# Down products with partial sums kept in PSUM, low parts of four passes on VectorE, and token block sums ordered a pair ahead

## The chip, the cores and the metric

The kernel runs on one core of a Trainium2 chip. The metric is the device time of one execution in microseconds (us). Five engines work side by side, each through its own queue in order: TensorE (PE in the rows; PEld is its weight load), VectorE (DVE), ScalarE (ACT), GpSimd (POOL) and SyncE (SP), which here issues the DMAs.

## The reference

A hybrid encoder layer is run on two request groups of 1024 tokens with the same weights. What matters here is its feed-forward end, per group:

```python
xn = rms_norm(h, norm_ffn_g[l])
g, u = jnp.split(xn @ w_gate_up[l], 2, axis=-1)      # 1024 x 1024 @ 1024 x 5632
h = h + (jax.nn.silu(g) * u) @ w_down[l]             # 1024 x 2816 @ 2816 x 1024
h = rms_norm(h, final_norm_g)
```

All is float32.

## The kernel before

**Products.** A float32 operand is split into a high part, rounded to the matmul's 32-bit format (`fp32r`), and a low part, the rest. `mm3` (line 430) makes one product of 128x128 by 128x512 out of three matmuls: high by high, high by low, low by high. ScalarE makes the high part (a CAST), VectorE or GpSimd the low part (a subtraction), both into one operand tile `wop`.

**Seven products for eight.** The gate and up products and the down products are cut into 2 x 2 blocks, and the four block results come from seven block products by Winograd's scheme. Its price is sums: of token blocks (`t23`, in `x_side`), of weight blocks, of hidden activation blocks `A[i, j, c]` (i the token half, j even or odd hidden tile), and of results.

**The down products.** `DN` lists the seven passes. A pass is 11 units (`c` from 0 to 10), one for each pair of hidden tiles of 128; a unit is four token quarters `q` by three matmuls, into the four PSUM banks of the pass, so 132 matmuls a pass. The banks of even and of odd passes alternate. When a pass is through, `C[p]` says into which blocks of `h` (token half, column half) its banks are added; `dn_unit` spreads these additions (`add`, VectorE, one 128x512 each, PSUM and SBUF in, SBUF out) over the units of the next pass, behind the quarters 1 and 3; in P3 at most two a unit. When none is left in P3, `T.d_free` is set, and the PSUM banks go to what follows: the transposes of the next group's tokens (`nx_trans`) in the first group, the final norms of the odd row tiles in the second.

**Operands of a unit.** `prep_dn` takes the sums of activation and weight blocks (VectorE; two of them by turns on VectorE and GpSimd, `turn`) and lets ScalarE make the two high parts, of the activation operand `sop` and the weight operand `top`. `prep_dn_lo` makes the low part of `top` on VectorE and that of `sop` on GpSimd. `prep(n)` is called ahead of unit n: it prepares further units as long as the operand tiles suffice (a ring of 7, 6 of them in use, 2 a unit, so up to unit n + 2), and then `lows(n + 2)` makes the low parts up to unit n + 1. That is the order in every engine's queue: sums and high parts of unit n + 2, low parts of unit n + 1, additions beside unit n. `trun` holds one block of `w_down` that is changed in place from pass to pass; `raws` holds the other blocks, loaded by SP into four buffers, each one when the load four before it is freed.

**Token block sums.** `x_side` is a generator that TensorE's program steps between groups of three matmuls of the first gate and up products. Of each of four token quarters it transposes blocks by TensorE (`x_trans`: four 128x128 transposes into one PSUM bank, then ScalarE's high part and VectorE's low part). B22 comes first; then, quarter by quarter, the sums `t23` (two VectorE operations, the second on the first), two GpSimd operations on `b21` and `b12`, and the transposes of T2, T3 and T4, T4 being the block that GpSimd wrote.

All instructions carry the line of the helper that emits them (line 120), so rows are told apart by tiles: `aA` to `aV` hold activation blocks, `wraw` a block of weights, `t` is `t23`, `x2n` the normed tokens.

Of the kernel before, what the change touches and what calls it, by code (L numbers as in the profile page):

```python
# [37 lines left out]
DN = ("P1", "P2", "P4", "P5", "P7", "P6", "P3")  # L38
# [208 lines left out]
def hymba_kernel(ctx, tc, ins, outs, dbg=None):  # L247
# [891 lines left out]
    def attention(T, b):  # L1139
# [341 lines left out]
        def x_side():  # L1481
# [37 lines left out]
            for q in range(4):  # L1519
                x_trans("B22", q, blocks(q)[3])  # L1520
                yield True
            for q in range(4):
                b11, b21, b12, b22 = blocks(q)
                t23 = slot(("s6", "s2")[q % 2], [P, 2, 512], name="t23")
                dve.tensor_tensor(t23[:, 1], b22, b12, ALU.subtract)
                dve.tensor_tensor(t23[:, 0], t23[:, 1], b11, ALU.add)
                yield True
                pool.tensor_tensor(b21, t23[:, 0], b21, ALU.subtract)
                pool.tensor_tensor(b12, b12, b11, ALU.subtract)
                x_trans("T2", q, t23[:, 0])  # L1530
                yield True
                x_trans("T3", q, t23[:, 1])
                yield True
                x_trans("T4", q, b21)
                yield True
# [76 lines left out]
    def ffn_stream(T, b):  # L1612
# [33 lines left out]
        two("P2", 1, L0)  # L1646
        for c in range(NC):
            items.append((("P4", c), [P, 2, 512], [(lambda r, i=i: r[:, i], rows(2 * c + i, L1)) for i in range(2)]))
        for c in range(NC):
            items.append((("P5", c), [P, 2, 512], [(lambda r: r.rearrange("p a b -> p (a b)"), rows(2 * c, slice(0, D)))]))  # L1650
        two("P6", 0, L0)
# [54 lines left out]
        def trun_tile(c):  # L1706
            if c % 2 == 0:
                trun[c // 2] = slot(trun_tags[c // 2], [P, 2, 512], name="trun")
                for i in range(min(2, NC - c)):
                    sync.dma_start(out=trun[c // 2][:, i], in_=rows(2 * (c + i), L0))  # L1710
# [6 lines left out]
        def prep_dn(p, c):  # L1717
            tr = trun[c // 2][:, c % 2]
            turn = (dve, pool)[c % 2]
            if p == "P1":  # L1720
                src, s = tr, A[1, 1, c]
            elif p == "P2":
                src, s = raws[(p, c - c % 2)][:, c % 2], A[1, 2, c]
                dve.tensor_tensor(tr, tr, src, ALU.subtract)
            elif p == "P4":
                r = raws[(p, c)]
                b12, b22 = r[:, 0], r[:, 1]
                dve.tensor_tensor(b22, b22, b12, ALU.subtract)
                turn.tensor_tensor(b12, b22, tr, ALU.add)
                src, s = b12, A[2, 2, c]  # L1730
            elif p == "P5":
                r = raws[(p, c)]
                dve.tensor_tensor(A[2, 2, c], A[2, 1, c], A[2, 2, c], ALU.add)
                dve.tensor_tensor(r[:, 0], r[:, 1], r[:, 0], ALU.subtract)
                src, s = r[:, 0], A[2, 2, c]
            elif p == "P7":
                dve.tensor_tensor(A[2, 1, c], A[1, 1, c], A[2, 1, c], ALU.subtract)
                src, s = tr, A[2, 1, c]
                dve.tensor_tensor(A[1, 1, c], A[2, 2, c], A[1, 1, c], ALU.subtract)
            elif p == "P6":  # L1740
                r = raws[(p, c - c % 2)]
                dve.tensor_tensor(tr, tr, r[:, c % 2], ALU.add)
                src, s = tr, A[1, 1, c]
            else:
                src, s = raws[(p, c - c % 2)][:, c % 2], A[1, 2, c]
# [5 lines left out]
            if p == "P6":  # L1751
                turn.tensor_tensor(A[1, 2, c], A[1, 2, c], A[1, 1, c], ALU.subtract)
            half[p, c] = src, s, sop, top

        def prep_dn_lo(p, c):
            src, s, sop, top = half.pop((p, c))
            dve.tensor_tensor(top[:, 1], src, fv(top[:, 0]), ALU.subtract)
            pool.tensor_tensor(sop[:, 1], s, fv(sop[:, 0]), ALU.subtract)
            ops["dn", p, c] = (q4((sop[:, 0], sop[:, 1])), (top[:, 0], top[:, 1]))
            if p in ("P2", "P6", "P3"):  # L1760
                if c % 2 or c == NC - 1:
                    freed.add((p, c - c % 2))
            elif p in ("P4", "P5"):
                freed.add((p, c))

# [34 lines left out]
    def ffn(T, b, nxt):  # L1800
# [112 lines left out]
        def gu_hook(p, t):  # L1913
# [5 lines left out]
            if p == "P1":  # L1919
                a_load(1, 1, 0, slot(xb[0], [P, 8, 512], name="aA"), 0, 8)  # L1920
# [272 lines left out]
```

## Time and profile before

| | us |
|---|---|
| median of 3 runs (lowest to highest) | 2489.55 (2488.89 to 2494.42) |
| the profiled execution | 2492.62 |
| its span, first to last instruction | 2490.8 |
| TensorE busy in it | 2356.5 |
| down products, first group | 1012.7 to 1252.0 |
| down products, second group | 2244.2 to 2476.5 |

Times in rows count from the start of the span. A matmul's listed duration overlaps the next one's, so the pace is read from starts: a unit of 12 matmuls takes about 2.8 us. The mean granted clock of TensorE is 0.983 of full speed.

### The profile page before, as it was taken

Reading aid. Unit: us, or ns where it says so; the run is one execution under the profiler, and the core shown is the slowest. Engines: PE = TensorE matmul, PEld = TensorE weight load, DVE = VectorE, ACT = ScalarE, POOL = GpSimd, SP = SyncE. Lnnn points to the kernel's source line nnn. Section 1 sums busy time; section 2 is a strip of 40 time slices with the busy share of each in tenths; the row PEclk is TensorE's granted clock in tenths of the full one; section 3 lists DMA queues with packets and bytes.
Section 4 is the critical chain, followed back from the end, with each engine's and each line's share of the span. In section 5 each row is a group of like instructions: output and inputs, shape, how many; then the busy total and the mean of one; then the engine's idle time right before and its main releaser. Section 6 shows DMA issues by size and latency. Waiting matters only on the chain. (4 is left out here: it accounts for less than half of the span.)

```text
span 2490.8 us, 34160 instructions
## 1 busy us (share of the span) xinstructions
PE 2356.5 (95%) x12458; PEld 1992.5 (80%) x12458; DVE 1775.0 (71%) x2472; ACT 1187.2 (48%) x2131; POOL 1256.0 (50%) x1156
## 2 busy tenths in 40 slices
PE   7998999998999999999989889999899999999997
PEld 7887899877888888777777789988778888887765
DVE  6686888876555555599966778888755555557996
ACT  4476667664232222343545766666532232223434
POOL 5323666544444444466663156665444444444665
PEclk9999999999999999999999999999999999999999
DMA  5113000111222222842430130001212223247513
GB/s 140 39 37 103 18 18 18 43 68 43 85 85 85 76 77 93 337 151 70 144 130 21 37 108 22 10 18 43 85 51 77 85 77 93 77 140 283 169 47 114
DMA packets 189704, 212.78 MB, mean 85 GB/s; under 512 B 24272, under 2 KB 141008, under 8 KB 188512
## 3 DMA queue, kind: packets, MB, share of 16 engines
q1 hardware_dynamic: 189536, 210.60, 26.1%
q8 instruction: 98, 1.61, 0.3%
q14 instruction: 70, 0.57, 0.1%
HBM read 168.45 MB, written 39.85 MB: 84 GB/s over the span
## 5 line engine op out<-in xcount | busy, mean ns | idle before, releaser
L120 PE MATMUL dn<-wop 128*128 128x512 f32 x1848 | 449.4, 401 | 17.7 <-DVE wop L120 14.5
L120 PEld LDWEIGHTS dn<-wop 128*128 128x128 f32 x1848 | 343.2, 189 | 117.0 <-DVE wop L120 36.4
L120 POOL TENSOR_TENSOR pexp<-pexp,rsum 128x1024 f32<-128x1024 f32 x128 | 242.9, 1898 | 230.6 <-DVE rsum L120 158.4
L120 PE MATMUL gu<-xT,wop 128*128 128x512 f32 x1344 | 352.1, 394 | 0.0
L120 POOL TENSOR_TENSOR wop<-wraw,wop 128x512 fp32r<-128x512 f32 x176 | 228.9, 1302 | 214.1 <-ACT wop L120 214.1
L120 PEld LDWEIGHTS gu<-xT,wop 128*128 128x128 f32 x1344 | 252.7, 188 | 57.9
L120 POOL TENSOR_TENSOR wop<-wsum,wop 128x512 fp32r<-128x512 f32 x126 | 163.1, 1294 | 256.1 <-ACT wop L120 256.1
L120 PE MATMUL gu<-xB,wop 128*128 128x512 f32 x1136 | 287.8, 396 | 0.7 <-DVE xB L120 0.6
L120 ACT CAST wop<-wraw 128x512 fp32r<-128x512 f32 x264 | 162.2, 617 | 208.7 <-DVE wraw L120 127.2
L120 PE MATMUL gu<-xH,wop 128*128 128x512 f32 x1056 | 254.8, 396 | 0.0
L120 PEld LDWEIGHTS gu<-xB,wop 128*128 128x128 f32 x1136 | 212.1, 188 | 47.9 <-ACT xB L120 1.1
L120 PEld LDWEIGHTS gu<-xH,wop 128*128 128x128 f32 x1056 | 198.1, 188 | 46.0
L120 ACT CAST pt<-ptp 128x512 fp32r<-128x512 f32 x256 | 148.9, 586 | 121.2 <-PE ptp L120 119.9
L120 DVE TENSOR_REDUCE m<-S 128x1 f32<-128x1041 f32 x128 | 158.1, 1235 | 56.2 <-PE S L120 55.4
L120 ACT ACTIVATE pexp<-S,m 128x1041 f32<-128x1041 f32 x128 | 145.0, 1133 | 67.4 <-DVE m L120 59.8
L120 DVE TENSOR_TENSOR pt<-ptp,pt 128x512 fp32r<-128x512 f32 x256 | 168.2, 681 | 5.3 <-ACT pt L120 4.3
L120 PE MATMUL ptp<-idf,pexp 128*128 128x128 f32 x1024 | 156.4, 277 | 10.2 <-DVE pt L120 6.6
L120 PE MATMUL pvo<-pt,vst 128*128 128x256 f32 x1024 | 155.3, 295 | 3.5 <-DVE attnT L120 3.5
L120 PE MATMUL S<-kh,qs 128*128 128x348 f32 (+1 forms) x384 | 137.5, 360 | 21.9 <-ACT pexp L120 15.6
L120 PEld LDWEIGHTS ptp<-idf,pexp 128*128 128x128 f32 x1024 | 126.0, 143 | 21.5 <-issue 7.9
L120 ACT CAST wop<-wsum 128x512 fp32r<-128x512 f32 x126 | 78.0, 619 | 135.2 <-DVE wsum L120 135.2
L120 DVE SCALAR_TENSOR_TENSOR act<-th,act 128x512 f32<-128x512 f32 x84 | 139.0, 1654 | 2.9
(292 smaller groups left out, 5186.0 us busy)
## 6 DMA issues: line engine op xcount, KB each, us to landing
wraw<-in_w_gate_up SPq DMA_DIRECT2D x176, 256.0 KB, 3.8
wraw<-in_w_down SPq DMA_DIRECT2D x110, 256.0 KB, 3.0
ad<-act SPq DMA_DIRECT2D x44, 512.0 KB, 3.5
wraw<-in_w_down SPq DMA_DIRECT2D x22, 512.0 KB, 3.3
wraw<-in_w_in SPq DMA_DIRECT2D x32, 256.0 KB, 3.6
hd<-h SPq DMA_DIRECT2D x16, 512.0 KB, 5.0
h<-hd SPq DMA_DIRECT2D x16, 512.0 KB, 10.2
out<-h SPq DMA_DIRECT2D x15, 512.0 KB, 2.8
```

What stands on the lines that cost most here:

```text
L120: return fn(*args, **kw)
```

## The change

The down products run in another order, P2, P1, P4, P6, P5, P7, P3, and three of them (P6, P7, P3: `onto`) start on the banks of the pass two before them and add to what stands there: P6 onto P1, P7 onto P1 + P6, P3 onto P5. `C` has fewer entries for that. The sums of activations and weights are arranged anew, all on VectorE; in P4, P5, P6 and P7 the low part of `sop` is VectorE's too, elsewhere GpSimd's. P2 now takes its weights from `trun`, which is loaded with the odd rows; P1 and P7 load the even ones. The first activations loaded are those of odd hidden tiles. In `x_side` the sums of quarter q + 1 are issued ahead of the transposes of quarter q. The diff; the loads of activations, which change places in it as their passes do, are left out:

```diff
--- before.py
+++ after.py
@@ -35,7 +35,7 @@
 GU = (("P1", "B11"), ("P6", "T2"), ("P2", "B21"), ("P7", "T3"), ("P5", "T1"), ("P4", "T4"), ("P3", "B22"))
 
 FIRST = {"A11": ("B11", "B12"), "A21": ("B11", "B12"), "A12": ("B21", "B22"), "A22": ("B21", "B22")}
-DN = ("P1", "P2", "P4", "P5", "P7", "P6", "P3")
+DN = ("P2", "P1", "P4", "P6", "P5", "P7", "P3")
 NC = NHT // 2
 
 GELU_A = 0.044715
@@ -1519,19 +1519,26 @@
             for q in range(4):
                 x_trans("B22", q, blocks(q)[3])
                 yield True
+            t23 = {}
+
+            def sums(q):
+                b11, b21, b12, b22 = blocks(q)
+                t = t23[q] = slot(("s6", "s2")[q % 2], [P, 2, 512], name="t23")
+                dve.tensor_tensor(t[:, 1], b22, b12, ALU.subtract)
+                dve.tensor_tensor(t[:, 0], t[:, 1], b11, ALU.add)
+                pool.tensor_tensor(b21, t[:, 0], b21, ALU.subtract)
+                pool.tensor_tensor(b12, b12, b11, ALU.subtract)
+
+            sums(0)
+            yield True
             for q in range(4):
-                b11, b21, b12, b22 = blocks(q)
-                t23 = slot(("s6", "s2")[q % 2], [P, 2, 512], name="t23")
-                dve.tensor_tensor(t23[:, 1], b22, b12, ALU.subtract)
-                dve.tensor_tensor(t23[:, 0], t23[:, 1], b11, ALU.add)
-                yield True
-                pool.tensor_tensor(b21, t23[:, 0], b21, ALU.subtract)
-                pool.tensor_tensor(b12, b12, b11, ALU.subtract)
-                x_trans("T2", q, t23[:, 0])
-                yield True
-                x_trans("T3", q, t23[:, 1])
-                yield True
-                x_trans("T4", q, b21)
+                if q < 3:
+                    sums(q + 1)
+                    yield True
+                for i, n in enumerate(("T2", "T3")):
+                    x_trans(n, q, t23[q][:, i])
+                    yield True
+                x_trans("T4", q, blocks(q)[1])
                 yield True
             while not T.b12_free:
                 yield False
@@ -1643,12 +1650,13 @@
                 items.append(((p, c), [P, 2, 512], [
                     (lambda r, i=i: r[:, i], rows(2 * (c + i) + j, cs)) for i in range(min(2, NC - c))]))
 
-        two("P2", 1, L0)
+        two("P1", 0, L0)
         for c in range(NC):
             items.append((("P4", c), [P, 2, 512], [(lambda r, i=i: r[:, i], rows(2 * c + i, L1)) for i in range(2)]))
+        two("P6", 0, L0)
         for c in range(NC):
             items.append((("P5", c), [P, 2, 512], [(lambda r: r.rearrange("p a b -> p (a b)"), rows(2 * c, slice(0, D)))]))
-        two("P6", 0, L0)
+        two("P7", 0, L0)
         two("P3", 1, L1)
         freed = set()
 
@@ -1707,7 +1715,7 @@
             if c % 2 == 0:
                 trun[c // 2] = slot(trun_tags[c // 2], [P, 2, 512], name="trun")
                 for i in range(min(2, NC - c)):
-                    sync.dma_start(out=trun[c // 2][:, i], in_=rows(2 * (c + i), L0))
+                    sync.dma_start(out=trun[c // 2][:, i], in_=rows(2 * (c + i) + 1, L0))
 
         T.trun_tile = trun_tile
 
@@ -1716,52 +1724,54 @@
 
         def prep_dn(p, c):
             tr = trun[c // 2][:, c % 2]
-            turn = (dve, pool)[c % 2]
-            if p == "P1":
-                src, s = tr, A[1, 1, c]
-            elif p == "P2":
-                src, s = raws[(p, c - c % 2)][:, c % 2], A[1, 2, c]
-                dve.tensor_tensor(tr, tr, src, ALU.subtract)
+            r = None if p == "P2" else raws[(p, c if p in ("P4", "P5") else c - c % 2)]
+            rc = None if p == "P2" else r[:, c % 2]
+            if p == "P2":
+                src, s = tr, A[1, 2, c]
+            elif p == "P1":
+                src, s = rc, A[1, 1, c]
             elif p == "P4":
-                r = raws[(p, c)]
                 b12, b22 = r[:, 0], r[:, 1]
                 dve.tensor_tensor(b22, b22, b12, ALU.subtract)
-                turn.tensor_tensor(b12, b22, tr, ALU.add)
+                dve.tensor_tensor(b12, b22, tr, ALU.add)
                 src, s = b12, A[2, 2, c]
+                if c >= NC // 2:
+                    dve.tensor_tensor(A[2, 1, c], A[2, 1, c], A[2, 2, c], ALU.add)
+            elif p == "P6":
+                if c < NC // 2:
+                    dve.tensor_tensor(A[2, 1, c], A[2, 1, c], A[2, 2, c], ALU.add)
+                dve.tensor_tensor(A[1, 1, c], A[2, 1, c], A[1, 1, c], ALU.subtract)
+                dve.tensor_tensor(tr, tr, rc, ALU.add)
+                src, s = tr, A[1, 1, c]
             elif p == "P5":
-                r = raws[(p, c)]
-                dve.tensor_tensor(A[2, 2, c], A[2, 1, c], A[2, 2, c], ALU.add)
                 dve.tensor_tensor(r[:, 0], r[:, 1], r[:, 0], ALU.subtract)
-                src, s = r[:, 0], A[2, 2, c]
+                dve.tensor_tensor(A[2, 2, c], A[2, 2, c], A[1, 1, c], ALU.subtract)
+                src, s = r[:, 0], A[2, 1, c]
             elif p == "P7":
-                dve.tensor_tensor(A[2, 1, c], A[1, 1, c], A[2, 1, c], ALU.subtract)
-                src, s = tr, A[2, 1, c]
-                dve.tensor_tensor(A[1, 1, c], A[2, 2, c], A[1, 1, c], ALU.subtract)
-            elif p == "P6":
-                r = raws[(p, c - c % 2)]
-                dve.tensor_tensor(tr, tr, r[:, c % 2], ALU.add)
-                src, s = tr, A[1, 1, c]
+                dve.tensor_tensor(rc, tr, rc, ALU.subtract)
+                dve.tensor_tensor(A[1, 1, c], A[1, 2, c], A[1, 1, c], ALU.subtract)
+                src, s = rc, A[2, 2, c]
             else:
-                src, s = raws[(p, c - c % 2)][:, c % 2], A[1, 2, c]
+                src, s = rc, A[1, 1, c]
             sop, top = op_tile(), op_tile()
             act.copy(sop[:, 0], s)
             act.copy(top[:, 0], src)
             if p == "P4":
                 act.copy(tr, r[:, 1])
-            if p == "P6":
-                turn.tensor_tensor(A[1, 2, c], A[1, 2, c], A[1, 1, c], ALU.subtract)
             half[p, c] = src, s, sop, top
 
         def prep_dn_lo(p, c):
             src, s, sop, top = half.pop((p, c))
             dve.tensor_tensor(top[:, 1], src, fv(top[:, 0]), ALU.subtract)
-            pool.tensor_tensor(sop[:, 1], s, fv(sop[:, 0]), ALU.subtract)
+            (dve if p in ("P4", "P5", "P6", "P7") else pool).tensor_tensor(sop[:, 1], s, fv(sop[:, 0]), ALU.subtract)
             ops["dn", p, c] = (q4((sop[:, 0], sop[:, 1])), (top[:, 0], top[:, 1]))
-            if p in ("P2", "P6", "P3"):
-                if c % 2 or c == NC - 1:
-                    freed.add((p, c - c % 2))
-            elif p in ("P4", "P5"):
+            if p == "P1":
+                tr = trun[c // 2][:, c % 2]
+                dve.tensor_tensor(tr, src, tr, ALU.subtract)
+            if p in ("P4", "P5"):
                 freed.add((p, c))
+            elif p != "P2" and (c % 2 or c == NC - 1):
+                freed.add((p, c - c % 2))
 
         n_lo = [0]
 
...
-        C = {"P1": ((1, 1, 1), (1, 2, 1), (2, 1, 1), (2, 2, 1)), "P2": ((1, 1, 1),), "P3": ((1, 2, 1),),
-             "P4": ((2, 1, -1),), "P5": ((1, 2, 1), (2, 2, 1)), "P6": ((1, 2, 1), (2, 1, 1), (2, 2, 1)),
-             "P7": ((2, 1, 1), (2, 2, 1))}
+
+        C = {"P2": ((1, 1, 1),), "P1": ((1, 1, 1),), "P4": ((2, 1, -1),), "P6": ((1, 2, 1),), "P5": ((2, 2, 1),),
+             "P7": ((2, 1, 1), (2, 2, 1)), "P3": ((1, 2, 1),)}
+        onto = ("P6", "P7", "P3")
         adds = []
         banks = {}
 
@@ -1963,11 +1974,11 @@
         def dn_unit(p, c):
             n = DN.index(p)
             if c == 0:
-                banks[n] = [bank(n % 2, q, "dn") for q in range(4)]
+                banks[n] = banks[n - 2] if p in onto else [bank(n % 2, q, "dn") for q in range(4)]
             (sh, sl), (th, tl) = ops.pop(("dn", p, c))
             due = -(-len(adds) // (NC - c)) if p != "P3" else min(2, len(adds))
             for q in range(4):
-                mm3(banks[n][q], sh[:, q], sl[:, q], th, tl, c == 0, c == NC - 1)
+                mm3(banks[n][q], sh[:, q], sl[:, q], th, tl, c == 0 and p not in onto, c == NC - 1, p in onto)
                 if q % 2 and due:
                     due -= 1
                     adds.pop(0)()
@@ -2059,10 +2070,10 @@
                     need(*guards[u])
                 elif T.x_in[guards[u][0]] < guards[u][1]:
                     return False
-            if u[0] == "dn" and u[1] == "P1":
-                return (1, 1, u[2]) in A
+            if u[0] == "dn" and u[1] == "P2":
+                return (1, 2, u[2]) in A
             if nxt is not None and u[0] == "dn":
-                if u[1:] == ("P6", NC - 3):
+                if u[1:] == ("P7", NC - 3):
                     T.no_rope = True
                 if u[1:] == ("P3", 1):
                     nxt_begin()
```

## Rows read from the trace of the kernel before

**Rows 1.** The page: busy us, share of the span and instructions of each engine.
```profile
PE 2356.5 (95%) x12458; PEld 1992.5 (80%) x12458; DVE 1775.0 (71%) x2472; ACT 1187.2 (48%) x2131; POOL 1256.0 (50%) x1156
```

**Rows 2.** Windows by pass: stretch, its us, busy us (instructions) by engine, clock, DMA share, GB/s.
```profile
core 0: us, PE busy (x) PEld busy (x) DVE busy (x) ACT busy (x) POOL busy (x), PEclk, DMA share, GB/s
...
1076.61:1109.58 32.97, 31.36 (x134) 24.60 (x132) 32.83 (x33) 16.70 (x30) 23.74 (x15) 1.00 0.49 161
1109.58:1141.54 31.96, 31.96 (x134) 23.97 (x132) 31.89 (x38) 13.48 (x23) 16.67 (x12) 1.00 0.55 179
1141.54:1178.41 36.87, 34.80 (x133) 25.10 (x132) 36.56 (x42) 13.30 (x24) 24.17 (x15) 0.95 0.05 16
1178.41:1211.74 33.33, 31.83 (x134) 24.27 (x132) 31.25 (x35) 12.13 (x21) 19.13 (x14) 1.00 0.34 111
...
2279.03:2309.60 30.57, 30.57 (x134) 24.81 (x132) 27.32 (x39) 13.61 (x24) 15.08 (x11) 1.00 0.50 188
2309.60:2342.49 32.89, 31.38 (x133) 24.58 (x132) 32.75 (x33) 16.71 (x30) 23.71 (x15) 1.00 0.50 160
2342.49:2374.45 31.96, 31.96 (x133) 24.01 (x132) 31.89 (x38) 13.47 (x23) 16.67 (x12) 1.00 0.55 180
2374.45:2409.80 35.35, 33.30 (x134) 23.96 (x132) 35.04 (x41) 13.08 (x24) 22.82 (x14) 1.00 0.01 2
2409.80:2445.80 36.00, 32.45 (x133) 24.13 (x132) 34.66 (x37) 12.78 (x23) 22.35 (x16) 1.00 0.24 81
```

**Rows 3.** Timeline of VectorE in P4, second group: start, us, operation, [idle before].
```profile
2317.12 0.67 DVE L120 TENSOR_TENSOR h<-h,dn 128x512 f32<-128x512 f32 x1
2317.72 0.68 DVE L120 TENSOR_TENSOR wraw<-wraw 128x512 f32<-128x512 f32 x1
2318.32 0.68 DVE L120 TENSOR_TENSOR wop<-wraw,wop 128x512 fp32r<-128x512 f32 x1
2318.92 0.68 DVE L120 TENSOR_TENSOR h<-h,dn 128x512 f32<-128x512 f32 x1
2319.52 1.18 DVE L120 TENSOR_TENSOR wraw<-wraw 128x512 f32<-128x512 f32 x1
2320.74 1.66 DVE L120 TENSOR_TENSOR wraw<-wraw,trun 128x512 f32<-128x512 f32 x1
```

**Rows 4.** Timeline of GpSimd in the same stretch.
```profile
2318.53 1.62 POOL L120 TENSOR_TENSOR wraw<-wraw,trun 128x512 f32<-128x512 f32 x1 [1.88 <-DVE wraw L120]
2320.11 1.73 POOL L120 TENSOR_TENSOR wop<-aC,wop 128x512 fp32r<-128x512 f32 x1
```

**Rows 5.** Timeline of VectorE and of ScalarE in P2, second group.
```profile
2293.82 0.69 DVE L120 TENSOR_TENSOR wop<-wraw,wop 128x512 fp32r<-128x512 f32 x1 [0.39 <-ACT wop L120]
...
2293.17 0.62 ACT L120 CAST wop<-wraw 128x512 fp32r<-128x512 f32 x1 [1.65 <-PE dn L120]
```

**Rows 6.** Timeline of TensorE at the start of the second group's down products.
```profile
2244.15 3.21 PE L120 MATMUL dn<-wop 128*128 128x512 f32 x13
2249.86 3.35 PE L120 MATMUL dn<-wop 128*128 128x512 f32 x7 [2.51 <-DVE wop L120]
```

**Rows 7.** Timeline of TensorE, VectorE, GpSimd at the token block sums.
```profile
574.71 0.63 PE L120 MATMUL tp<-idf,t 128*128 128x128 f32 x4 [1.42 <-DVE t L120]
...
591.86 0.63 PE L120 MATMUL tp<-idf,t 128*128 128x128 f32 x4 [1.41 <-DVE t L120]
...
1823.82 0.63 PE L120 MATMUL tp<-idf,t 128*128 128x128 f32 x4 [1.41 <-DVE t L120]
...
573.88 0.69 DVE L120 TENSOR_TENSOR t<-t,x2n 128x512 f32<-128x512 f32 x1
...
574.71 1.28 POOL L120 TENSOR_TENSOR x2n<-t,x2n 128x512 f32<-128x512 f32 x1 [4.28 <-DVE t L120]
```

**Rows 8.** Timeline of TensorE around the end of the first group's P3.
```profile
1228.74 0.60 PE L120 MATMUL tp<-idf,xn 128*128 128x128 f32 x4
...
1255.37 0.47 PE L120 MATMUL pin<-xsXH,whi 128*128 128x512 f32 x1 [3.42 <-DVE h L120]
```

**Rows 9.** Timeline of VectorE behind the last matmul.
```profile
2479.13 2.47 DVE L120 SCALAR_TENSOR_TENSOR h<-h,rs,gfin 128x1024 f32<-128x1024 f32 x2
2482.32 1.28 DVE L120 SCALAR_TENSOR_TENSOR h<-h,rs,gfin 128x1024 f32<-128x1024 f32 x1 [0.72 <-POOL rs L120]
```

More of the change, by code (lines that the diff above doesn't have):

```diff
@@ L1919, in gu_hook @@
             if p == "P1":
-                a_load(1, 1, 0, slot(xb[0], [P, 8, 512], name="aA"), 0, 8)
+                a_load(1, 2, 0, slot(xb[0], [P, 8, 512], name="aA"), 0, 8)
                 T.trun_tile(2)
@@ L1923, in gu_hook @@
                 hold["B"] = slot(xb[1], [P, 8, 512], name="aB")
-                a_load(1, 1, 8, hold["B"], 0, 2)
+                a_load(1, 2, 8, hold["B"], 0, 2)
             elif p == "P2":
@@ L1933, in gu_hook @@
                 hold["V"] = v4
-                a_load(1, 2, 0, w, 0, 2)
-                a_load(1, 2, 2, s7, 0, 2)
+                a_load(1, 1, 0, w, 0, 2)
+                a_load(1, 1, 2, s7, 0, 2)
             elif p == "P3":
@@ L1938, in gu_hook @@
                     T.trun_tile(c)
-                a_load(1, 1, 10, hold["B"], 2, 1)
+                a_load(1, 2, 10, hold["B"], 2, 1)
                 k4, s5 = (slot(x, [P, 2, 512], name="aS") for x in (S_K, "s5"))
-                a_load(1, 2, 4, k4, 0, 2)
-                a_load(1, 2, 6, s5, 0, 1)
-                a_load(1, 2, 7, hold["V"], 0, 4)
+                a_load(1, 1, 4, k4, 0, 2)
+                a_load(1, 1, 6, s5, 0, 1)
+                a_load(1, 1, 7, hold["V"], 0, 4)
                 h = T.h = slot("H", [P, TT, D], name="h")
```

## The prediction

> **What bounds the kernel now.** I read the page first: TensorE is busy for 95% of the span, VectorE for 71% [rows 1]. So a gain can come only from the places where TensorE waits, or runs slower than its clean pace. The change touches two stages, the down products (seven passes of 11 units, 132 matmuls a pass) and the token block sums in front of the gate and up products, so I cut these stages out: a table of windows by pass for the first, the timeline for the second.
>
> The passes [rows 2]. P2 of the second group runs without a wait: 30.57 us, 2.78 a unit. I take that as the clean pass (the same pass of the first group took 30.49); four of them are 122.2. The passes P4, P5, P7, P6 take 32.97 + 31.96 + 36.87 + 33.33 = 135.1 us in the first group and 32.89 + 31.96 + 35.35 + 36.00 = 136.2 in the second: 12.9 and 14.0 too much. In each of the eight, VectorE is busy nearly as long as the pass (31.89 of 31.96 in P5), while TensorE has idle time: VectorE is the bound there.
>
> But is it by its own work? Its timeline says no [rows 3]. While GpSimd stands still, one VectorE operation of 128x512 starts every 0.60 us (2317.12, 2317.72, 2318.32, 2318.92), though each is listed with 0.67 to 0.68. At 2318.53 GpSimd starts [rows 4]; the VectorE operation at 2319.52, with both inputs in SBUF, now takes 1.18 instead of 0.68: the GpSimd one ends at 2318.53 + 1.62 = 2320.15, and VectorE's 0.55 later, as if it had waited for that end. The next one, beside the GpSimd operation of 2320.11, takes 1.66. The two engines take turns. In P5 of the second group 38 operations fill 31.89 us, 0.84 each; without turns they would be 38 x 0.60 = 23. An addition that reads PSUM (`h<-h,dn`) isn't lengthened.
>
> **The change part by part.** *Fewer additions.* With the sums kept in PSUM, the list of additions to `h` shrinks from 14 block products x 4 = 56 to 8 x 4 = 32 a group. At 0.60 that is 14 us of VectorE a group, no time of TensorE by itself.
>
> *Low parts on VectorE.* In P4, P6, P5, P7 GpSimd loses all it did there: 44 low parts and 10 sums a group. VectorE gets them. Its operations in these four passes, by the new `prep_dn`: P4 22 sums, 6 of A, 22 low parts; P6 5 + 22 and 22; P5 and P7 22 and 22 each; 16 additions to `h`. That is 203 operations a group. At 0.60 they are 122 us, against 122.2 of the clean matmuls: by the whole, a draw. So order decides. An operation that reads what the one before it wrote starts 0.04 after the listed end (2319.52 + 1.18, then 2320.74 [rows 3]): 0.72 for the first of such a pair.
>
> By the order written, a step holds the sums of two units on, the low parts of the next, and one addition in the first four steps. In P4: 0.72 + 0.60 + 1.20 + 0.60 = 3.12 for three steps, 3.72 for the fourth (the A sum starts at c = 5), then 3.12, where the last two hold P6's sums: 34.9 us against 30.6, so 4.3 short. In P6: 0.72 + 1.20 + 1.20 + 0.60 = 3.72 for three steps, 3.00 for one, then 2.40: short by 3 x 0.94 + 0.22 = 3.0, then faster than TensorE by 0.38 a step. In P5 and P7: 3.00 for four steps (0.9 short in all), then 2.40.
>
> What covers this is VectorE's lead. In P2's pass it works as far ahead as the ring of operand tiles lets it: ScalarE's copy at 2293.17 had waited for TensorE, and the low part behind it starts at 2293.82 after 0.39 of idle time [rows 5]. By the units of 2.78 from 2279.03, the fifth unit had then just ended; the ring gives its tile to the unit three on, the eighth, which starts at 2298.5. So a low part is ready 4.0 us early. P4 uses that up and lacks 0.3 to 0.6; P6 pays its 3.0 in full; P5 and P7 live on the regained lead. Loss: 3.6 us a group, so 125.8 for the four. Bounds: nothing (122.2), and 8 if there is no lead at all. Gain: 135.1 - 125.8 = 9.3 and 136.2 - 125.8 = 10.4, together **19.7**, bounds 11 and 27.
>
> *The moved waits.* P6, P7 and P3 start onto banks that VectorE has to have read; those additions lie in the first four units of the pass between, seven units earlier: nothing. If VectorE were seven units late, that would be priced above already. P7 loads B11 a second time, 11 blocks of 256 KB a group on SP's queue; in the pass P7 of before the DMA engines are busy for 0.01 of the time [rows 2], and each load waits for a raw buffer four loads back, so nothing. The stop of 2.51 us in the second unit of the whole stage [rows 6] is VectorE's and GpSimd's turns at the end of the gate products; P2 as first pass has the same operations as P1 had, and I leave it at zero, between -2 and +2.
>
> *Token block sums.* Before, each of the four sums of a group is issued right ahead of the transposes that need it: TensorE stands for 1.42 us until the second of the two dependent VectorE operations is done [rows 7]; four times in each group, the first and the last shown. After, a sum is issued three or four transposes ahead. Only the first has no lead, but one step of three matmuls (3 x 2.78 / 12 = 0.7) more in front of it: about 0.7 of its 1.42 stays. Gain 4 x 1.42 - 0.7 = 5.0 a group, **10.0**; bounds 6 and 11.4. What could be late next is the third transpose of each four, which reads a GpSimd result: it ended 574.71 + 1.28 - 574.57 = 1.4 after its sum, with VectorE taking turns perhaps 2.0 (1.73 there [rows 4], against 1.28 here), and the third transposes come three steps, 2.1, and two transposes after that: still in time.
>
> *The two ends.* With 8 instead of 12 additions at two a unit the banks for what follows come free after four units of P3 and not after six, 5.6 us earlier. In the first group the transposes of the next group's tokens start at 1228.74 and the next products wait 3.42 us for the last additions [rows 8]; VectorE would then reach those additions sooner. I take **2.5**, between 0 and 5: it can't be more than the wait and the small stops around it. In the second group the odd rows are finished earlier, and the row of two operations at 2479.13 [rows 9] holds one fewer: **0.9**, between 0 and 1.5.
>
> The sum: 19.7 + 10.0 + 2.5 + 0.9 = **33.1 us**. The profiled execution took 2492.62, so 2459.5; it is 3.1 above the median of the runs, from which it would be 2456.5. I take **2458**.
>
> A rule against this: the Trainium skill, "VectorE: DVE Perf Modes", section "The DRAIN you can't avoid", says that the next operation starts only when the pipe of the one before is empty (a section beside it lets some start earlier). By it an operation would cost its whole listed time, and the trace doesn't agree: 0.68 listed, 0.60 from start to start. It is the first rival.
>
> **The rivals.**
> - *VectorE at its listed time.* 203 operations at 0.68 are 138.0 a group; less the 4.0 of lead, 134.0 against 135.1 and 136.2. The passes give 3 us, the rest stands: 2492 - 17 = about 2475. For it: the listed durations, and that many of the new operations have another order than the ones read. Against it: every undisturbed row.
> - *Slower: a chain of waits.* VectorE has to wait for ScalarE's copy between sums and low parts. If it does so with its lead gone, every operation costs 0.72 or more, as the dependent pair does, and there is no lead: 2 x 146.2 against 271.3 is 21 more, less 13.4 from the other parts: 8 slower, **2498**. It decides from 0.70 us an operation on. For it: P4 and P6 run without lead for ten steps. Against it: between a unit's sums and its low parts stand the low parts of another, 1.2 us or more, and ScalarE's two copies are 1.05.
> - *The sums bring nothing,* since the third transpose then waits for GpSimd, whose operations take turns with the sum ahead: 10 less, 2468. Against it: the 2.0 against over 2.1 above; it is close, so the chance isn't small.
> - *No loss in the passes and all ends at their best:* 2445 to 2448.
> - *The change doesn't do what it says* (low parts still on GpSimd) is excluded by the code for P4 to P7; P2, P1 and P3 keep theirs.
>
> **How the numbers follow.** The forecast 0.66; the sums bring nothing 0.12; the best case 0.08; listed time 0.07; the chain of waits 0.07. The range takes the first three and part of the fourth: 2445 to 2477. A change under 0.2% (5 us) is about what a measurement of this kernel can't tell from none. Slower: the chain and a little for what I don't see, 0.08. Same: 0.04, the upper end of listed time. Faster: 0.88.
>
> **What would show it.** After: the passes P4, P6, P5, P7 at about 31, 33.5, 30.6, 30.6 with GpSimd idle in them; VectorE starts 0.60 apart; TensorE's stops, if any, in the first units of P6 and waiting for VectorE; no 1.42 before the transposes but a 0.7 in front of the first; transposes in P3 from its fifth unit on. Wrong if P5 and P7 take over 31.5 (VectorE is slower than 0.60), or if transposes wait for GpSimd.

## The result and the profile after

| | before | changed |
|---|---|---|
| median of 4 runs, us | 2489.22 (2488.33 to 2494.42) | 2458.85 (2456.95 to 2461.70) |
| ratio to before | 1 | 0.9877, 95% interval 0.9864 to 0.9889 |
| span of the profiled execution, us | 2490.8 | 2458.2 |

The kernel is 30.4 us faster; 2458 was forecast. First the windows by pass of the changed kernel, as in [rows 2]: P4, P6 of the first group (P5 and P7 took 30.52 and 30.55), then P4, P6, P5, P7 of the second.

```profile
core 0: us, PE busy (x) PEld busy (x) DVE busy (x) ACT busy (x) POOL busy (x), PEclk, DMA share, GB/s
...
1071.39:1103.09 31.70, 31.47 (x133) 24.50 (x132) 31.35 (x51) 16.76 (x30) 0.00 (x0) 1.00 0.51 170
1103.09:1136.75 33.66, 32.65 (x133) 24.33 (x132) 33.55 (x57) 14.24 (x24) 0.00 (x0) 1.00 0.31 101
...
2287.40:2319.09 31.69, 31.49 (x133) 24.50 (x132) 31.34 (x52) 16.78 (x30) 0.00 (x0) 1.00 0.50 166
2319.09:2352.79 33.70, 32.73 (x133) 24.34 (x132) 33.60 (x57) 14.21 (x24) 0.00 (x0) 1.00 0.31 99
2352.79:2383.39 30.60, 30.60 (x134) 24.80 (x132) 30.11 (x51) 12.59 (x22) 0.00 (x0) 1.00 0.55 177
2383.39:2414.01 30.62, 30.62 (x133) 24.80 (x132) 25.12 (x41) 12.59 (x22) 4.41 (x3) 1.00 0.28 95
```

GpSimd is idle in three of the four passes and starts in P7 only with P3's low parts. VectorE does more operations in less time: 57 in 33.70 us of P6, where 41 took 35.35 in P7 before. P5 and P7 run at TensorE's clean pace. The loss that is left stands in P4 and P6, and VectorE is busy for the whole of both.

The timeline of VectorE in P6 of the second group, and the two stops of TensorE that answer to it:

```profile
2322.81 0.68 DVE L120 TENSOR_TENSOR h<-h,dn 128x512 f32<-128x512 f32 x1
2323.41 0.69 DVE L120 TENSOR_TENSOR aD<-aD,aC 128x512 f32<-128x512 f32 x1
2324.13 0.69 DVE L120 TENSOR_TENSOR aS<-aD,aS 128x512 f32<-128x512 f32 x1
2324.74 0.69 DVE L120 TENSOR_TENSOR trun<-trun,wraw 128x512 f32<-128x512 f32 x1
2325.34 0.69 DVE L120 TENSOR_TENSOR wop<-trun,wop 128x512 fp32r<-128x512 f32 x1
2325.94 0.69 DVE L120 TENSOR_TENSOR wop<-aS,wop 128x512 fp32r<-128x512 f32 x1
2326.55 0.68 DVE L120 TENSOR_TENSOR h<-h,dn 128x512 f32<-128x512 f32 x1
```

```profile
2326.08 3.44 PE L120 MATMUL dn<-wop 128*128 128x512 f32 x12 [0.31 <-DVE wop L120]
2329.82 4.57 PE L120 MATMUL dn<-wop 128*128 128x512 f32 x16 [0.30 <-DVE wop L120]
```

One step of P6 is six operations: 2326.55 - 2322.81 = 3.74 us. From start to start they take 0.60, and 0.72 where the next one reads what this one wrote (2323.41 to 2324.13). TensorE's two stops are 2329.82 - 2326.08 = 3.74 apart too: the step of VectorE has become the step of the unit.

The other places, each the answer to rows of before: the first transposes of the token block sums in the first group [rows 7], the next products behind the first group's P3 [rows 8], the rows behind the last matmul [rows 9], and the start of the down products [rows 6].

```profile
573.46 0.63 PE L120 MATMUL tp<-idf,t 128*128 128x128 f32 x4 [0.73 <-DVE t L120]
...
1239.24 0.47 PE L120 MATMUL pin<-xsXH,whi 128*128 128x512 f32 x1 [0.87 <-DVE h L120]
...
2447.36 1.28 DVE L120 SCALAR_TENSOR_TENSOR h<-h,rs,gfin 128x1024 f32<-128x1024 f32 x1 [0.19 <-POOL rs L120]
2449.65 1.29 DVE L120 SCALAR_TENSOR_TENSOR h<-h,rs,gfin 128x1024 f32<-128x1024 f32 x1 [1.00 <-POOL rs L120]
...
2229.11 2.13 PE L120 MATMUL dn<-wop 128*128 128x512 f32 x8 [2.52 <-DVE wop L120]
```

Of four stops of 1.42 one is left in each group, of 0.73 in the first and 0.75 in the second. The products behind P3 wait 0.87 and not 3.42. The row of two operations behind the last matmul is one of one. The stop at the start of the down products is as it was.

### The profile page after: what moved, and what is told of

It is laid out like the page before. It is cut to its first block, busy times and chain, and to the rows that moved or that the text cites. A ratio compares the mean times of both kernels' runs of the same rounds, so it can differ in the third digit from the quotient of the medians.

```text
span 2458.2 us, 34049 instructions
## 1 busy us (share of the span) xinstructions
PE 2345.8 (95%) x12458; PEld 1992.9 (81%) x12458; DVE 1748.4 (71%) x2554; ACT 1189.0 (48%) x2131; POOL 1090.5 (44%) x1048
## 5 line engine op out<-in xcount | busy, mean ns | idle before, releaser
L120 PE MATMUL dn<-wop 128*128 128x512 f32 x1848 | 441.0, 397 | 8.2 <-DVE wop L120 6.9
L120 ACT CAST wop<-wraw 128x512 fp32r<-128x512 f32 x286 | 176.3, 619 | 271.1 <-DVE wraw L120 136.6
L120 POOL TENSOR_TENSOR wop<-aS,wop 128x512 fp32r<-128x512 f32 x28 | 41.2, 1472 | 289.6 <-ACT wop L120 288.4
```

Of the source, the lines that this page charges most:

```text
L120: return fn(*args, **kw)
```

## The experiments

Three things were open behind a right sum: whether the passes gained by the low parts or by the sums kept in PSUM; whether VectorE's time per step is what is left in P4 and P6; and what the stop at the start, left at zero, comes from. Each run has its own whole time beside runs of the kernel before on the same chip. But stages that no edit touches differ between executions: in the profiles shown here and below the first product of the output projection starts anywhere from 259.7 to 265.8 us. And the kernel orders TensorE's instructions, while it is built, by an estimate of their times (`Plan`), so an edit in one stage can change the order of instructions in another. So an effect of a few us is read from the windows of the stage itself.

**The token block sums in their old place.**

```diff
...
-            sums(0)
-            yield True
...
-                if q < 3:
-                    sums(q + 1)
-                    yield True
...
+            for q in range(4):
...
+                dve.tensor_tensor(t23[:, 1], b22, b12, ALU.subtract)
+                dve.tensor_tensor(t23[:, 0], t23[:, 1], b11, ALU.add)
+                yield True
...
```

> The changed kernel with the token block sums in their old place, right ahead of the transposes that need them. My theory (TensorE stands until the second of two dependent VectorE operations is done): the stop of 1.4 us comes back four times a group in place of one of 0.73, so 2 x 4.9 = 9.9 us more than the changed kernel, 2469. The rival (TensorE is only early and waits as long further on): no stop is won by the order, 2459.

Measured: 2475.03, ratio to before 0.9946 (0.9929 to 0.9964), 16 more than the changed kernel and not 10. The stops are back:

```profile
573.13 0.63 PE L120 MATMUL tp<-idf,t 128*128 128x128 f32 x4 [1.42 <-DVE t L120]
```

Windows of this run, and then of the changed kernel, say where the 16 are: the first gate and up products of the first group (first line of each; in the second group they take 56.90 and 52.40), and the stage behind the first group's P3, whose code the edit doesn't touch (second line).

```profile
564.10:621.00 56.90, 51.19 (x260) 41.08 (x261) 33.25 (x53) 22.89 (x41) 29.43 (x23) 1.00 0.16 47
1243.10:1452.10 209.00, 183.90 (x996) 157.34 (x996) 143.20 (x178) 118.40 (x212) 80.31 (x88) 0.94 0.20 61
```

```profile
564.40:615.80 51.40, 50.62 (x261) 41.33 (x261) 35.58 (x53) 22.95 (x41) 30.59 (x23) 1.00 0.17 52
1239.20:1442.70 203.50, 182.63 (x996) 156.70 (x996) 134.51 (x176) 119.11 (x212) 80.84 (x88) 0.96 0.20 63
```

The sums cost 5.5 and 4.5, together 10.0, as expected. Another 5.5 us lie in the second stage, with the same number of matmuls, 996. There TensorE runs at the lower of its two levels, 1.2 and not 2.4 GHz, for a longer time: the granted clock is 0.94 in the mean in place of 0.96. That can't be all. The run with the low part ahead of the gate, further below, has 0.94 there too and takes 203.50, as long as the changed kernel:

```profile
1235.50:1439.00 203.50, 184.16 (x996) 158.02 (x996) 134.48 (x176) 118.89 (x212) 80.89 (x88) 0.94 0.21 63
```

What sets the run with the old sums apart is the order of the matmuls. In the changed kernel TensorE turns to the products `gp` 1.0 us after a wait in this stage, in the run with the old sums 6.1 us after it, with 15 `pin` matmuls in place of 2 ahead (the changed kernel first):

```profile
1292.91 0.77 PE L120 MATMUL pin<-xsXH,whi 128*128 128x512 f32 x1 [5.17 <-DVE kropet L120]
...
1293.90 0.21 PE L120 MATMUL gp<-ch,gwt 128*128 128x16 f32 x1
```

```profile
1296.96 0.77 PE L120 MATMUL pin<-xsXH,whi 128*128 128x512 f32 x1 [6.47 <-DVE kropet L120]
...
1303.02 0.17 PE L120 MATMUL gp<-ch,gwt 128*128 128x16 f32 x1
```

With the old sums TensorE is busy for only 1.3 us more (183.90 and 182.63), the rest is waiting, and VectorE is busy for 143.20 in place of 134.51. The kernel before and all other runs but the next one have the changed kernel's order in this stage, and take 200.7 to 206.0 for it. The 209.0 lies 3.0 above all of them. So at least that much goes with another order of the same work, and not with the stops at the sums; which wait it comes from wasn't tried.

**All low parts of the activation operand back on GpSimd.**

```diff
-            (dve if p in ("P4", "P5", "P6", "P7") else pool).tensor_tensor(sop[:, 1], s, fv(sop[:, 0]), ALU.subtract)
+            pool.tensor_tensor(sop[:, 1], s, fv(sop[:, 0]), ALU.subtract)
```

> The changed kernel with all low parts of the activation operand back on GpSimd. My theory (VectorE's operations with two SBUF inputs and GpSimd's take turns, about 1.1 us of VectorE for each GpSimd operation, as in the P5 of before with its step of 2.91): steps of 3.6 in P4, 2.9 to 4.2 in P6, 2.9 to 3.5 in P5 and P7, so the four passes take about 141 us a group where the changed kernel takes 126.5, 29 us more in all, 2488. The rival (what counts is the number of VectorE's own operations, 159 in place of 203 a group, 95 us at 0.60): the four passes come down to the clean 122, 2450.

Measured: 2484.81, ratio 0.9983 (0.9972 to 0.9995). Windows of P4, P6, P7, second group:

```profile
2298.84:2335.31 36.47, 32.20 (x134) 24.26 (x132) 36.12 (x43) 16.16 (x30) 16.70 (x10) 1.00 0.47 158
2335.31:2372.19 36.88, 32.80 (x134) 23.96 (x133) 36.78 (x44) 14.81 (x25) 18.74 (x13) 1.00 0.25 79
...
2405.10:2437.38 32.28, 31.19 (x133) 24.56 (x132) 29.33 (x35) 12.57 (x22) 17.19 (x12) 1.00 0.27 94
```

138.5 us for the four against 126.6, with fewer operations of VectorE (43 and 52 in P4); that is even more than the 136.2 of before, so part of what the token block sums gain is lost again. The theory of turns holds, its price of 141 was 2 to 3 too high; the rival's 122 is out.

**The kernel before, with the low parts on VectorE and nothing else.**

```diff
-            pool.tensor_tensor(sop[:, 1], s, fv(sop[:, 0]), ALU.subtract)
+            (dve if p in ("P4", "P5", "P6", "P7") else pool).tensor_tensor(sop[:, 1], s, fv(sop[:, 0]), ALU.subtract)
```

> The kernel before with one edit: in P4, P5, P6 and P7 the low part of the activation operand is made by VectorE. My theory (turns with GpSimd are nearly all of the loss in the passes): VectorE has 190 operations a group in the four passes, 114 us at 0.60, and no step falls short by more than its lead; the passes go from 135 and 136 to about 123, 25 us less than the kernel before, 2464, without any sum kept in PSUM. The rival (the 24 additions a group that PSUM saves are needed to make room): the passes stay at 33 us and more, 2484 to 2489.

Measured: 2470.67, ratio 0.9928 (0.9911 to 0.9945), between the two. Windows of P4, P5, P7, P6, second group, and the timelines of VectorE and GpSimd in the one pass that isn't clean:

```profile
2293.77:2324.36 30.59, 30.59 (x133) 24.80 (x132) 30.45 (x44) 17.51 (x31) 6.18 (x4) 1.00 0.56 178
2324.36:2354.98 30.62, 30.62 (x134) 24.81 (x132) 30.52 (x49) 13.74 (x23) 1.68 (x1) 1.00 0.56 184
2354.98:2390.53 35.55, 32.21 (x134) 24.32 (x133) 35.27 (x51) 12.67 (x22) 6.66 (x4) 1.00 0.03 11
2390.53:2421.15 30.62, 30.62 (x133) 24.80 (x132) 28.02 (x45) 12.57 (x22) 3.89 (x3) 1.00 0.24 85
```

```profile
2379.78 0.69 DVE L120 TENSOR_TENSOR wop<-trun,wop 128x512 fp32r<-128x512 f32 x1
2380.39 1.77 DVE L120 TENSOR_TENSOR wop<-aB,wop 128x512 fp32r<-128x512 f32 x1
...
2379.95 1.66 POOL L120 TENSOR_TENSOR aV<-aV,aB 128x512 f32<-128x512 f32 x1 [5.68 <-DVE aB L120]
```

Three passes are clean without any sum kept in PSUM. In P7 GpSimd does what belongs to P6, the next pass: `aV<-aV` is the sum of A[1, 2], which the old code gives by turns to GpSimd. With the low parts gone its queue holds nothing else, so each such sum runs as soon as its input is there, a pass early, and VectorE's operation beside it takes 1.77 in place of 0.69. That I had not seen in the code.

**The same, with the sums by turns on VectorE as well.**

```diff
-            turn = (dve, pool)[c % 2]
+            turn = dve
```

> The kernel before with the low parts of P4, P5, P7 and P6 on VectorE and with the sums that went by turns to GpSimd on VectorE as well. My theory (in the run with the low parts alone, GpSimd, freed of them, ran ahead to the next pass's sums and so took turns with VectorE in P7): P7 goes from 35.6 to about 30.6, at most 1 us is lost in P6, 4 to 5 us a group less than that run, 2462. The rival (P7 stops since VectorE has 52 operations there): P7 stays at 33 to 35 us, 2468 to 2471.

Measured: 2461.89, ratio 0.9892 (0.9876 to 0.9909). P7 and P6, second group:

```profile
2353.88:2384.47 30.59, 30.59 (x133) 24.80 (x132) 30.31 (x50) 13.08 (x22) 0.00 (x0) 1.00 0.05 16
2384.47:2415.18 30.71, 30.71 (x134) 24.73 (x133) 29.12 (x48) 12.57 (x22) 5.71 (x3) 1.00 0.23 79
```

All four passes take 122.5 us, 4.1 less than in the changed kernel, with the old order and all 56 additions. So in the old order the passes gain by GpSimd's absence alone.

**The changed kernel with fresh banks and 56 additions.**

```diff
-        C = {"P2": ((1, 1, 1),), "P1": ((1, 1, 1),), "P4": ((2, 1, -1),), "P6": ((1, 2, 1),), "P5": ((2, 2, 1),),
-             "P7": ((2, 1, 1), (2, 2, 1)), "P3": ((1, 2, 1),)}
-        onto = ("P6", "P7", "P3")
+        C = {"P1": ((1, 1, 1), (1, 2, 1), (2, 1, 1), (2, 2, 1)), "P2": ((1, 1, 1),), "P3": ((1, 2, 1),),
+             "P4": ((2, 1, -1),), "P5": ((1, 2, 1), (2, 2, 1)), "P6": ((1, 2, 1), (2, 1, 1), (2, 2, 1)),
+             "P7": ((2, 1, 1), (2, 2, 1))}
+        onto = ()
```

> The changed kernel with fresh banks for P6, P7 and P3, and so all 56 additions a group. My theory (VectorE's time in each pass, at 0.60 an operation): P4 with 16 additions in place of 4 goes to about 38 us, P6 stays at 33.7, P5 with 12 goes to 31.3, P7 with 8 to 32: 8.6 us a group more than the changed kernel, 2476. The rival (additions read PSUM and cost the passes nothing, since VectorE's stops in P6 have another cause): 2459.

Measured: 2477.93, ratio 0.9955 (0.9940 to 0.9969). P4 and P7, second group:

```profile
2293.32:2330.98 37.66, 33.98 (x134) 24.25 (x132) 37.31 (x62) 16.15 (x29) 0.00 (x0) 1.00 0.41 140
...
2396.45:2429.32 32.87, 32.87 (x134) 24.02 (x132) 31.28 (x51) 12.57 (x22) 5.71 (x3) 1.00 0.26 88
```

37.7 for the 38 expected, 32.9 for 32; P6 took 34.88 and P5 30.59, where 33.7 and 31.3 were expected. The four passes take 136.0 against 126.6, 9.4 a group where 8.6 was expected. That is as long as the 136.2 of before, with GpSimd out of the way: in the new order both are needed, GpSimd's absence (138.5 with its low parts back) and the sums in PSUM (136.0 without them). The sums pay for what the new order brings into these passes: without them 40 additions a group fall there, in the old order 24, and the eleven A sums come on top.

**The A sums spread.** Seven of them are issued in P1 and four in P4.

```diff
+                if c >= 4:                                   # P1
+                    dve.tensor_tensor(A[2, 1, c - 4], A[2, 1, c - 4], A[2, 2, c - 4], ALU.add)
-                if c >= NC // 2:                             # P4
+                if c >= 7:
-                if c < NC // 2:                              # P6
-                    dve.tensor_tensor(A[2, 1, c], A[2, 1, c], A[2, 2, c], ALU.add)
```

> The changed kernel with the eleven sums of A[2, 1] and A[2, 2] issued in other places: seven in P1 from its fifth unit on, four in P4 from its eighth, none in P6. My theory (the stops at the end of P4 and in the first units of P6 are VectorE's time, 3.7 us a step against TensorE's 2.8): P4 goes from 31.7 to 30.6 and P6 from 33.7 to 30.6, 4.2 us a group, 2450 or about 8 under the changed kernel. The rival (P6 stops because it adds onto the banks of P1, or because of its two-step operands): P6 stays at 33.7, 2458.

Measured: 2457.84, ratio 0.9875 (0.9860 to 0.9890): no gain that can be told. P1, P4, P6 of the second group, and VectorE in P1:

```profile
2253.58:2286.18 32.60, 31.36 (x134) 24.50 (x132) 28.61 (x37) 13.56 (x24) 12.14 (x8) 1.00 0.48 178
2286.18:2318.51 32.33, 31.99 (x133) 24.36 (x132) 32.02 (x53) 16.98 (x31) 0.00 (x0) 1.00 0.53 180
2318.51:2349.12 30.61, 30.61 (x133) 24.80 (x132) 30.61 (x52) 13.99 (x23) 0.00 (x0) 1.00 0.34 110
```

```profile
2261.52 0.92 DVE L120 TENSOR_TENSOR aD<-aD,aC 128x512 f32<-128x512 f32 x1 [3.92 <-DMA aD<-ad]
```

P6 is clean, adding onto P1's banks as ever: the rival is out, its stops were VectorE's time. But the gain of 3.1 went back: 2.0 into P1, where VectorE waits 3.92 for A[2, 1], the last of the activations to land, and 0.6 into P4, which starts without its lead.

**The low part ahead of the gate.** At the last gate unit the low parts of one more unit are issued.

```diff
-            lows(n + 2)
+            lows(n + 2 + (n + 1 < len(T.units) and T.units[n][0] == "gu" and T.units[n + 1][0] == "dn"))
```

> The changed kernel with the low parts of the second down unit issued one step earlier, ahead of the last gate product's results in VectorE's queue. My theory (the stop of 2.5 us in the second unit of the down products is the place in VectorE's queue: behind the gate's last operations, each taking turns with GpSimd): the first pass goes from 33.4 (35.0 where the clock falls to its half) to 30.6, 6 to 7 us in all, 2452. The rival (the low part would have to wait for GpSimd or ScalarE there too, or the gate's chain, pushed back, holds up the third unit): the stop moves and the time stays, 2458.

Measured: 2450.47, ratio 0.9843 (0.9829 to 0.9858). The first pass of both groups:

```profile
1006.34:1036.98 30.64, 30.64 (x133) 24.75 (x132) 16.66 (x17) 13.54 (x24) 16.58 (x12) 1.00 0.87 326
2217.69:2248.38 30.69, 30.69 (x134) 24.75 (x133) 16.65 (x17) 13.55 (x24) 16.54 (x12) 1.00 0.87 339
```

They took 34.95 and 33.45: 7.1 us less. The stop was the place in VectorE's queue.

**These two and an earlier first sum together** (`sums(0)` ahead of the third transpose of B22).

> The changed kernel with both edits of the runs beside it, and with the first token block sum issued two transposes earlier. If the three places are independent: 8 and 6 to 7 and 1.5 us (twice the stop of 0.73) under the changed kernel, 2442. If they draw on the same lead of VectorE, the sums in P1 and P4 come too late again and P4 and P6 keep half of their stops: 2446 or more.

Measured: 2456.12, ratio 0.9867 (0.9852 to 0.9882), worse than the one edit alone. P1 of the second group, and VectorE in it:

```profile
2247.25:2283.11 35.86, 32.19 (x134) 25.77 (x132) 28.75 (x39) 13.60 (x24) 13.36 (x8) 0.95 0.55 205
```

```profile
2258.27 0.69 DVE L120 TENSOR_TENSOR aD<-aD,aC 128x512 f32<-128x512 f32 x1 [7.00 <-DMA aD<-ad]
```

Without the stop of the first pass P1 comes earlier, the transfer doesn't, and the wait grows from 3.92 to 7.00 (in the first group from 1.95 to 5.94). P1 takes 35.86 and in the first group 37.07, and the mean clock in it falls to 0.95 and 0.91. Neither case that I wrote down was this one.

**Both orders with all of it.** The changed kernel has three of the A sums late in P1 and eight in P4, the low part ahead and the early first sum. The kernel before has VectorE in GpSimd's place, the new `x_side` with the early first sum, and the low part ahead; nothing is kept in PSUM.

> The changed kernel with the same two edits of order and with the eleven sums of A[2, 1] spread so that none is asked for before its data have landed: three in P1 from the ninth unit, eight in P4 from the fourth. My theory (P4 short by 4.3 against a lead of 4.0, P6 by 0.9, the stop on the landing of the last activations gone): 1.2 us a group left of 4.2, so from the run with the low part ahead (2450.5) 6 less and 1.5 for the first sum, 2443. The rival (the transfer of the last activations still holds VectorE up in P1): P1 over 31 us and 2448 or more.

> The kernel before, with its order of passes and its sums in h, and four edits: low parts and by-turns sums of P4, P5, P7, P6 on VectorE, token block sums a pair ahead with the first one two transposes earlier, and the second down unit's low parts ahead of the gate's last results. My theory (each place counted by itself): from the run without GpSimd's part (2461.9) 10 us for the token block sums, 1 for the first of them, 5.6 for the first pass, 2445, with nothing kept in PSUM. The rival (sums in PSUM are needed for the last microseconds, since without the stop of the first pass VectorE's 56 additions come closer together): 2450 or more.

Measured, beside the same runs of before (2491.46): the changed order 2443.38, ratio 0.9807 (0.9793 to 0.9820); the old order 2439.38, ratio 0.9800 (0.9784 to 0.9816). The two intervals overlap, so the whole times don't say which order is faster. P4 of the changed order, then P4 of the old one, second group (its P5, P7 and P6 took 30.62, 30.59 and 30.62):

```profile
2278.87:2311.81 32.94, 32.24 (x133) 24.34 (x132) 32.66 (x54) 16.97 (x30) 0.00 (x0) 1.00 0.49 162
```

```profile
2269.43:2300.03 30.60, 30.60 (x133) 24.80 (x132) 30.06 (x50) 17.31 (x31) 0.00 (x0) 1.00 0.59 191
```

In the old order every pass is clean, with 48 to 51 operations of VectorE each. In the changed order P4 loses 2.3 where I had expected 0.3, for two reasons. The sum of two units on is what a step holds, so the eight A sums start at the second step and not at the fourth: after nine steps VectorE is 4.8 behind (one of 3.12, three of 3.72, five of 3.12, against nine units of 2.78), not 4.3. And VectorE enters P4 with a lead of 2.3, not 4.0: the last low part of its first unit is ready at 2276.54, and the unit starts at 2278.87. From 4.8 less 2.3 comes 2.5, an estimate.

But the old order loses at the ends. From the start of P3 to the next products, first group, the changed order and then the old one:

```profile
1190.10:1231.40 41.30, 38.78 (x198) 30.57 (x196) 36.96 (x46) 29.02 (x52) 24.60 (x26) 1.00 0.39 141
```

```profile
1183.70:1227.77 44.07, 39.27 (x197) 30.50 (x196) 39.36 (x50) 29.46 (x52) 26.74 (x26) 0.99 0.36 127
```

That is 2.8 more, and 0.9 more from the start of the last P3 to the end of the span (45.0 and 44.2). P4 gives the old order 4.8 in the two groups, the ends take 3.7 of it back. So which of the two is faster stays open; what is shown is that the old order comes as far with nothing kept in PSUM. By the medians both are faster than the changed kernel, by 15 and 19 us.

## Why the prediction was right

- **The bound.** That the passes were held by VectorE taking turns with GpSimd, not by VectorE's own work: shown from both sides, by the run with the low parts back (138.5 us for four passes) and by the old kernel without GpSimd (122.5). The Trainium skill, "SBUF — State Buffer", section "Who interferes with whom", has it that a VectorE instruction with two SBUF inputs contends with a GpSimd instruction that reads SBUF. The trace agrees: 1.77 us beside a GpSimd operation of 1.66, 0.69 without one. One reading beside it was wrong: in P5 TensorE is not idle but listed as busy for all of the 31.96 [rows 2]; the loss there is a slower pace.
- **0.60 us an operation.** Held, 0.72 for a dependent pair too, in rows of new operations. The first rival, the listed time, would have made the 62 operations of P4 in the run without sums in PSUM 42 us; the pass took 37.7. The rule of the Trainium skill, "VectorE: DVE Perf Modes", section "The DRAIN you can't avoid", is that the next operation does not start until the pipe is empty, and that one which is not held starts earlier. These rows show the second: listed at 0.68, they start 0.60 apart.
- **The loss of 3.6 a group in P4 and P6.** It is 126.4 - 122.1 = 4.3 and 126.6 - 122.2 = 4.4, in the steps named: 3.74 us in the first units of P6, forecast 3.72. The term was 0.7 to 0.8 too small, most of it in P4, which lost 1.2 and 1.1 where 0.3 to 0.6 was reckoned. What was mis-sized is the lead. VectorE in P1 and P4 of the second group, the low part of P1's tenth unit, the first sum for P4, and the last low part of P4's first unit:

```profile
2277.20 0.69 DVE L120 TENSOR_TENSOR wop<-wraw,wop 128x512 fp32r<-128x512 f32 x1 [0.38 <-ACT wop L120]
...
2279.53 0.68 DVE L120 TENSOR_TENSOR wraw<-wraw 128x512 f32<-128x512 f32 x1
...
2284.00 0.68 DVE L120 TENSOR_TENSOR wop<-aC,wop 128x512 fp32r<-128x512 f32 x1
```

P1's tenth unit starts at about 2281.9, so the lead is still 4.0 there. P4's first unit starts at 2287.40, so P4 begins with 2.7. The sums of P4's first two units fall, beside P1's own operations, into the last two steps of P1, and the prediction had counted them nowhere. With 2.7 its own 4.3 would have left 1.6, an estimate. The passes gave 8.7 + 9.6 = 18.3, forecast 19.7.
- **The token block sums.** 4.9 in each group from the rows, forecast 5.0; the first sum's rest 0.73 and 0.75, forecast 0.7. No third transpose waited for GpSimd.
- **The start of the stage.** The stop was left at zero and stayed (2.52). That the clock's fall behind it now struck the first group's pass (34.95, mean clock 0.95) and not the second's was worth nothing in sum. As an opportunity it was missed: the prediction put the stop down to turns with GpSimd, and with one low part moved ahead of the gate's last operations in VectorE's queue the pass takes 30.64; one line takes 7 us out.
- **The two ends.** From the start of P3 to the next products 43.6 before and 41.4 after, 2.2, forecast 2.5. From the start of the last P3 to the end of the span 45.0 and 44.2, 0.8, forecast 0.9; the last unit lost some of it, with a stop of 0.64 for a low part behind a final norm. That the smaller number of additions is the reason isn't shown: the run with fresh banks has 8 behind P7 as well, and took 45.3 in the first group.
- **The sum.** 18.3 + 9.9 + 2.2 + 0.8 = 31.2 of 32.6 us between the two spans; 1.3 of the rest lie ahead of the first gate product, in code that is the same (565.7 and 564.4). So the forecast of 33.1 was 1.9 too high, nearly all of it in the passes, and that 2458 was met within 1 us is in part luck: it had been taken between what the profiled execution and the median gave, and by the medians the gain is 30.4.

What the prediction did not ask is whether the new order was needed. It counted the additions saved as room for the low parts. In the new order that is so (136.0 without them, 126.6 with them); in the old order the room is there without it: VectorE has 200 operations in the four passes with everything on it, in the new order 203.

## What to carry to other kernels

Before work is given to a second engine, look at what the first one's operations cost beside it: here an operation on GpSimd took about 1.1 us from the VectorE operation beside it (1.77 - 0.69), and about 0.8 on the average of the four passes of before (136.2 us less 149 operations at 0.60, over 57 of GpSimd; an estimate), more than the 0.60 it saved. When one engine is the bound, count its operations step by step against its lead and not over the stage: 203 operations a group fit exactly, and yet the uneven ones cost 4.4 us, where 200 even ones cost nothing. And when a stop is taken out, ask which transfer the work behind it will now meet. Where a program orders its instructions by an estimate of its own, an edit can move a stage that it doesn't touch: compare the order there before the chip is held responsible.

## What the runs showed of the hardware that I had not expected

- An engine whose queue has been thinned runs far ahead: GpSimd did sums a whole pass (some 30 us) early, as soon as their input was there, and disturbed a pass to which they don't belong (35.6 us and not 30.6).
- How long a stage takes at a given order of its work varies, and the mean clock tells only a part: the 996 matmuls behind the first group's P3 took, in the changed kernel's order, 200.7 to 203.5 us at a mean granted clock of 0.96 (five profiles) and 203.5 to 206.0 at 0.94 (four). The 209.0 at 0.94 was another order.
